# Delta rule of block 2: four inverse chains in other places, the second pair on other banks, more products queued at the start of the mixers

## The chip, the cores and the metric

One core of one Trainium2 chip runs the whole program, two transformer blocks, in one launch. The metric is device time in microseconds, the median of the runs of one kernel. The traces name the engines PE (matmul), DVE (vector), ACT (scalar), POOL (GpSimd) and SP (which issues DMAs).

## The reference, cut to what matters

Block 1 (a token mixer and sixteen experts) and the experts of block 2 are not touched. The change lies in the mixing sublayer of block 2, on 256 rows of width 1024:

```python
u_lat = modulate(rmsnorm(h_lat, norm_mix_g), m_lat[0], m_lat[1])
a_lat, b_lat, gates_lat = jnp.split(u_lat @ w_in, split_at, axis=-1)
oa = gdn_branch(a_lat, state_a, ...)      # gated delta rule, 4 heads of 128, two directions
ob = rwkv_branch(b_lat, state_b, ...)     # 8 heads of 64, two directions
y  = sigmoid(g_a) * (oa @ w_o_a) + sigmoid(g_b) * (ob @ w_o_b)
return y @ w_out
```

The delta rule is computed in chunks of 128 rows; each head and direction has two chunks:

```python
lower = where(strict, (k_beta @ k.T) * decay, 0)
a_mat = eye(128) + lower                  # its inverse is applied to the right-hand sides
for each chunk, in the direction's order:
    v_new = u_c - w_c @ s                 # u, w come from the inverse
    o_c   = q_dec @ s + qk @ v_new
    s     = s * g_end + k_dec.T @ v_new
o = rmsnorm(o_fwd + o_bwd, onorm_g) * silu(z)
```

## The kernel before

Block 2's mixers stand in one stretch, between the context's part and the merge. Three streams of work share PE there.

**rwkv** (tiles r...) goes through four head pairs, j = 0 to 3. Each has a front (products `rmt`, then two inverses, `r0ic`/`r0ib`/`r0iy` and `r1ic`/`r1ib`/`r1iy`, one for each direction) and a back, a chain of small chunk steps (`rp`), in which each step reads the state `rSU` that DVE wrote after the last; then `rbn`, `ryt`, `rgb` close the pair. Its tiles lie in the pools R and RF, its banks of PSUM are pa, pc and pd.

**gdn**, the delta rule (tiles g...), has two pairs of heads. For a pair it makes transposes and products (`gtr`, `gkk`, `gqp`, `grb`), then for each direction an inverse of seven levels: four with 32x32 blocks (`gic`, two groups of products a level: PE, then a copy or subtraction on ACT or DVE, then PE again) and two with whole tiles (`gib`, `giy`, a copy on ACT and a subtraction on DVE between), and then two state steps (`gp`), each with five groups of products that go from PE to DVE and back (`gr`, `gvn`) before the state `SA` is written. Before, pair 0 runs its two directions one after the other, both with the tiles of the pool G, and pair 1 runs them in turn, direction 0 in G and direction 1 in the pool X. X is opened when RF is closed, so it lies in RF's memory, which is free once the last rwkv pair has had its last use of it. All of gdn takes its banks from pb (two of them).

**products** are input projections that depend on nothing of the two: `gz` (the gate z of the delta rule) and sixteen columns of `pc` with the sigmoids `early` (the gates g_a and g_b). They wait in the list `waiting[1]`; `waiting[0]` holds rwkv's next pair. `advance` takes steps from a list, and `fill` does so behind a given matmul; how many steps is in the table `HOPS`. `HOPS[6]` and `HOPS[7]` are the fillers of the delta rule's inverse and state steps; before, they act on direction 0 of pair 1 only (`both and d == 0`).

The program order is rwkv whole, then gdn whole, with the fillers where the hooks put them; a scheduler then merges this into one order for each engine, which is fixed at build time. Each engine keeps its order and waits at the head of its queue. This is why gdn's pair 0, written behind all of rwkv, stands among rwkv's products in the kernel before: its places (G, pb) are free early.

**merge** follows: SP loads `w_o_b`, `w_o_a` and `w_out` (L1891), ACT and DVE or POOL split each into two parts `wp` (L290, L291), and PE makes `mo` (w_o_b half by half, L300), `gr`, `mo` again (w_o_a) and `mw` (w_out). The experts follow with 366 GB/s of weights. The normed output of the delta rule reaches the merge through `gdn_out`: ACT squares (`gjk`, `goss`), DVE scales, PE transposes (`got`). 

Of the kernel before, what the change touches and what calls it, by code (L numbers as in the profile page):

```python
# [16 lines left out]
P = 128  # L17
# [41 lines left out]
HOPS = 4, 1, (3, 1), (2, 1), (2, 1), (2, 1), (0, 4), (0, 4)  # L59
# [95 lines left out]
class Ring(list):  # L155
# [3 lines left out]
    def tile(self, *args, **kw):  # L159
        self.turn += 1  # L160
        return self[self.turn % len(self)].tile(*args, **kw)


class Net:
# [796 lines left out]
    def ctx_pre(self):  # L961
# [6 lines left out]
        with tc.tile_pool(name="CW", bufs=2, reuse_waits="tile") as CW, tc.tile_pool(name="C", bufs=1, reuse_waits="tile") as C:  # L968
# [22 lines left out]
            with tc.tile_pool(name="CG", bufs=1, reuse_waits="tile") as G:  # L991
                gates = yield from self.gdn_gates(G, uT)
                for hp in range(2):
                    qkv = []
                    yield from self.gdn_in(G, uT, False, hp, load, qkv)
                    x = yield from self.gdn_products(G, qkv, False)
                    for d in range(2):
                        yield from self.gdn_dir(G, d, False, 2 * hp, gates, x, self.SA, False, None)
# [261 lines left out]
    def gdn(self, W, gates, ins, S, o, X):  # L1260
# [80 lines left out]
    def gdn_dir(self, W, d, both, h0, gates, x, S, lat, o):  # L1341
# [8 lines left out]
        hop = (lambda *steps: (lambda ins: self.fill(ins, *steps))) if both and d == 0 else lambda *steps: (lambda ins: None)  # L1350
# [32 lines left out]
        yield from self.mixed_inverse(W, u4(N), 4, d, u4(Y), 7, "gi", hop(*HOPS[6]))  # L1383
        sl = S[d][:, h0:h0 + 2, :]
        for step in range(2):
# [5 lines left out]
            hop(*HOPS[7])(ins)  # L1391
# [7 lines left out]
            hop(*HOPS[7])(ins)  # L1399
# [4 lines left out]
            if lat:  # L1404
                p3 = half("gp3")
                for h in range(2):
                    nc.tensor.matmul(p3[:, h, :], qd[:, t, h, :], sl[:, h, :], start=True, stop=False)
                    nc.tensor.matmul(p3[:, h, :], qk[:, t, h, :], vn[:, h, :], start=False, stop=True)
                ov = o[:, t, h0 * P:(h0 + 2) * P].rearrange("p (h c) -> p h c", h=2)
                if (step if both else d) == 0:  # L1410
                    nc.scalar.copy(ov, p3)
                else:
                    nc.vector.tensor_add(ov, ov, p3)
# [9 lines left out]
    def rwkv(self, W, F, uT, S, lat, load, tags, start=None):  # L1423
# [91 lines left out]
        start()  # L1515
        for j in range(4):
# [244 lines left out]
    def lat(self):  # L1761
        tc, nc, I = self.tc, self.nc, self.I
        h = self.acc
        with ExitStack() as outer:
            L = outer.enter_context(tc.tile_pool(name="L", bufs=1, reuse_waits="tile"))
            early = [L.tile([P, KD, 256], F32, name=f"early{i}", tag=f"exp{i}") for i in range(2)]
            with self.phase(**LBANKS):
# [31 lines left out]
                with tc.tile_pool(name="R", bufs=1, reuse_waits="tile") as R, tc.tile_pool(name="G", bufs=1, reuse_waits="tile") as G, ExitStack() as mix:  # L1799
# [62 lines left out]
    def gdn_out(self, W, sz, go, oa):  # L1862
        nc = self.nc
        ss = W.tile([P, 2, 4, 2], F32, name="goss")
        for t in range(2):
            jk = W.tile([P, P], F32, name="gjk", tag="gr", padded_shape=[P, 256])
            for hh in range(4):
                nc.scalar.activation(jk, go[:, t, hh * P:(hh + 1) * P], AF.Square, accum_out=ss[:, t, hh, 0:1])
            self.rsqrt_cols(ss[:, t, :, 1], ss[:, t, :, 0], 1.0 / P, self.eps)
            for hh in range(4):  # L1870
                c = slice(hh * P, (hh + 1) * P)
                nc.vector.scalar_tensor_tensor(go[:, t, c], go[:, t, c], ss[:, t, hh, 1:2],
                                               sz[:, t, c], op0=ALU.mult, op1=ALU.mult)
        for hh in range(4):
            b = self.bank("got")
            for t in range(2):
                nc.tensor.transpose(b[:, t * P:(t + 1) * P], go[:, t, hh * P:(hh + 1) * P], self.ident)
            self.evac(oa[:, hh, :], b[:, :256], self.pc("gdn_onorm_g_2"))
# [424 lines left out]
```

## Time and profile before

| | us |
|---|---|
| median of 3 runs (lowest, highest) | 2464.67 (2458.88, 2468.92) |
| the profiled execution, whole | 2459.26 |
| its span on the core | 2457.4 |
| mixers, rwkv pairs 0 to 2 with most of gdn pair 0 (A, 1764.67 to 1969.84) | 205.17 |
| mixers, rwkv pair 3 with gdn pair 1's start (B, to 2054.90) | 85.06 |
| mixers, end of gdn pair 1, last products (C, to 2112.49) | 57.59 |
| merge up to the experts (to 2177.00) | 64.51 |

Outside the span lie 1.86 us of the profiled execution. A, B and C are cut at events of the trace: A begins where the mixers' orders begin to differ, B with the front of rwkv's pair 3, C behind its last state step, and 2112.49 is the first `mo`.

The profile is read from the whole to the part: busy shares and the granted TensorE clock by slice first, then the windows of the four stages, then in each stage what PE waited for and what its groups cost, and last the single rows in order of time. A matmul in 32-bit floats shows as two records, so that counts of the trace are twice those of the order. Matmuls overlap in the pipeline: the price of a group in a row is taken from start to start.

### The profile page before, as it was taken

Reading aid. Unit: us, or ns where it says so; the run is one execution under the profiler, and the core shown is the slowest. Engines: PE = TensorE matmul, PEld = TensorE weight load, DVE = VectorE, ACT = ScalarE, POOL = GpSimd, SP = SyncE. Lnnn points to the kernel's source line nnn. Section 1 sums busy time; section 2 is a strip of 40 time slices with the busy share of each in tenths; the row PEclk is TensorE's granted clock in tenths of the full one; section 3 lists DMA queues with packets and bytes.
Section 4 is the critical chain, followed back from the end, with each engine's and each line's share of the span. In section 5 each row is a group of like instructions: output and inputs, shape, how many; then the busy total and the mean of one; then the engine's idle time right before and its main releaser. Section 6 shows DMA issues by size and latency. Waiting matters only on the chain. (4 is left out here: it accounts for less than half of the span.)

```text
span 2457.4 us, 45180 instructions
## 1 busy us (share of the span) xinstructions
PE 2280.8 (93%) x18736; PEld 1238.1 (50%) x18736; DVE 979.8 (40%) x2419; ACT 652.7 (27%) x1652; POOL 353.7 (14%) x627
## 2 busy tenths in 40 slices
PE   7989799999999999899999999987989989989997
PEld 6756433444444443333343333325867868865554
DVE  7735311223233133232222232215576663545545
ACT  5414111211211222111122121104444433422222
POOL 3101000000000111011011011003253431300000
PEclk9989899999999999999999999998979989999999
DMA  7637999999999999999999999994211104689995
GB/s 257 213 115 262 356 395 402 402 407 406 398 400 395 366 391 405 406 408 405 406 406 404 406 407 408 406 398 115 79 39 47 52 22 145 202 278 366 366 368 181
DMA packets 318816, 755.06 MB, mean 307 GB/s; under 512 B 12944, under 2 KB 158016, under 8 KB 315536
## 3 DMA queue, kind: packets, MB, share of 16 engines
q1 hardware_dynamic: 317104, 747.67, 81.2%
q0 software_dynamic: 1504, 4.46, 0.5%
q8 instruction: 150, 2.46, 0.4%
q14 instruction: 58, 0.48, 0.1%
HBM read 751.03 MB, written 1.05 MB: 306 GB/s over the span
## 5 line engine op out<-in xcount | busy, mean ns | idle before, releaser
L909 PE MATMUL gu<-w,xs 128*64 128x512 f32 (+1 forms) x3072 | 677.7, 569 | 22.8 <-DMA w<-in_w_up 18.6
L909 PEld LDWEIGHTS gu<-w,xs 128*64 128x64 f32 x3072 | 197.1, 137 | 326.5 <-issue 257.4
L941 PE MATMUL dn<-w,hT 128*64 128x512 f32 x1408 | 336.3, 602 | 21.4 <-DMA w<-in_w_down 20.7
L1110 PE MATMUL pc<-luT,w 128*128 128x256 f32 x688 | 177.2, 399 | 2.2 <-DMA w<-in_w_in 1.5
L941 PEld LDWEIGHTS dn<-w,hT 128*64 128x64 f32 x1408 | 88.4, 136 | 176.6 <-issue 118.2
L1110 PEld LDWEIGHTS pc<-luT,w 128*128 128x128 f32 x688 | 127.3, 195 | 19.5 <-issue 1.5
L2159 PE MATMUL egu<-w,exs 128*64 128x256 f32 x1024 | 123.2, 383 | 0.0
L2159 PEld LDWEIGHTS egu<-w,exs 128*64 128x64 f32 x1024 | 74.6, 136 | 39.4 <-issue 6.9
L1692 POOL TENSOR_SCALAR rsw<-rSU,rwc 64x64 f32<-64x64 f32 x112 | 39.6, 354 | 379.1 <-DVE rSU L1708 368.9
L919 DVE TENSOR_TENSOR hid<-hid,gu 128x512 f32<-128x512 f32 (+1 forms) x48 | 30.9, 643 | 123.4 <-ACT hid L307 123.2
L920 DVE TENSOR_TENSOR hid<-hid,gu 128x512 f32<-128x512 f32 (+1 forms) x48 | 30.8, 642 | 120.4 <-PE gu L909 120.3
L1110 PE MATMUL pc<-cuT,w 128*128 128x256 f32 x288 | 71.1, 391 | 0.0
L305 ACT ACTIVATE hid<-gu 128x512 f32<-128x512 f32 (+1 forms) x48 | 26.9, 560 | 163.6 <-PE gu L909 163.4
L2186 PE MATMUL edn<-w,ehT 128*64 128x512 f32 x256 | 67.7, 597 | 0.7 <-ACT ehT L322 0.5
L1110 PEld LDWEIGHTS pc<-cuT,w 128*128 128x128 f32 x288 | 52.1, 190 | 30.8 <-issue 20.4
L291 DVE TENSOR_TENSOR wp<-w,wp 128x1024 fp32r<-128x1024 f32 (+1 forms) x44 | 57.8, 1332 | 24.2 <-ACT wp L290 24.2
L1700 DVE COPY rSU<-rp 64x64 f32<-64x64 f32 x64 | 13.5, 214 | 134.5 <-PE rp L1696 134.2
L300 PE MATMUL pj<-uTh,wp 128*128 128x272 f32 x320 | 66.0, 299 | 0.0
L1648 PE MATMUL rmt<-rT,rBK 128*128 128x128 f32 (+1 forms) x256 | 50.9, 340 | 15.3 <-DVE rT L1635 7.3
L290 ACT CAST wp<-w 128x1024 fp32r<-128x1024 f32 (+1 forms) x48 | 55.0, 1187 | 29.8 <-DMA w<-in_w_in 17.8
L1193 DVE TENSOR_TENSOR r0iB<-r0iB,r0ic 128x128 f32<-128x128 f32 x48 | 13.6, 284 | 118.5 <-PE r0ic L1172 107.2
L958 DVE SCALAR_TENSOR_TENSOR acc<-sc,aff,acc 128x512 f32<-128x512 f32 x64 | 43.7, 744 | 37.9 <-PE sc L956 37.7
(675 smaller groups left out, 3514.5 us busy)
## 6 DMA issues: line engine op xcount, KB each, us to landing
w<-in_w_down SPq DMA_DIRECT2D x176, 1024.0 KB, 16.5
w<-in_w_gate SPq DMA_DIRECT2D x128, 1024.0 KB, 17.6
w<-in_w_up SPq DMA_DIRECT2D x128, 1024.0 KB, 18.1
w<-in_w_gate SPq DMA_DIRECT2D x64, 768.0 KB, 15.8
w<-in_w_up SPq DMA_DIRECT2D x64, 768.0 KB, 14.9
w<-in_moe_w_gate SPq DMA_DIRECT2D x32, 1024.0 KB, 13.3
w<-in_moe_w_up SPq DMA_DIRECT2D x32, 1024.0 KB, 12.3
w<-in_moe_w_down SPq DMA_DIRECT2D x32, 1024.0 KB, 11.3
```

The lines of the kernel that those rows point to most:

```text
L290: self.nc.scalar.copy(hi, src)
L291: (eng or self.nc.vector).tensor_sub(lo, src, hi)
L300: self.nc.tensor.matmul(out, a[x], b[y], start=(i == 0 and x + y == 0), stop=(i == n - 1 and x == 1))
L909: ins = nc.tensor.matmul(b[h * 64:(h + 1) * 64, :w], xs[:, k, :], ws(k, slice(h * w, (h + 1) * w)), start=(k == 0), stop=(k == KD - 1))
L919: nc.vector.tensor_mul(hid, hid, gu[0][:, :w])
L941: ins = nc.tensor.matmul(dn[0][dc * 64:(dc + 1) * 64], hT[:, j, h * 64:(h + 1) * 64], wd(h * nf + j, slice(dc * 512, (dc + 1) * 512)), sta ...
L958: nc.vector.scalar_tensor_tensor(dst, b, self.aff[:, t + 1, e:e + 1], dst, op0=ALU.mult, op1=ALU.add)
L1110: self.nc.tensor.matmul(b, w(k), uT[:, k, :], start=(k == 0), stop=(k == KD - 1))
L1648: ins = nc.tensor.matmul(b[:, i], BK[:, c0 + i, h:h + 2, :], T[:, h, c0 + i, :, :], start=True, stop=True)
L1692: nc.gpsimd.tensor_scalar(sw[r], SU[r, h, c, :], wc[r, c:c + 1], 0.0, op0=ALU.mult, op1=ALU.add)
L2159: nc.tensor.matmul(b[64 * i:64 * i + 64, x * 256:x * 256 + 256], xs[:, k, i, :], w[i](k), start=(k == 0), stop=(k == KD - 1))
L2186: nc.tensor.matmul(b[64 * i:64 * i + 64, :], hT[:, j, 64 * i:64 * i + 64], wd[i](j, cs), start=(j == 0), stop=(j == 1))
```

## The change

`HOPS[0]` goes from 4 to 12 and is now used: right after the mixers' beginning twelve steps of the products' list are queued. Both pairs of gdn run their two directions in turn. Pair 0 has direction 0 in G and direction 1 in X, on the banks pb, with (0, 2) fillers in direction 0; pair 1 puts its tiles by the class `Places` into places of rwkv's pool R (and five tiles into X), on the banks pa and pc, with (0, 4) fillers as before. `gdn_out` is done pair by pair, and the transposes `got` come behind both.

```diff
-HOPS = 4, 1, (3, 1), (2, 1), (2, 1), (2, 1), (0, 4), (0, 4)
+HOPS = 12, 1, (3, 1), (2, 1), (2, 1), (2, 1), (0, 2), (0, 4)
...
+class Places:
+    COMMON = dict(gkq=("R", "rT1", [P, 3, 2, 2, P]), gkN=("X", "xkN", None), gvN=("X", "xvN", None))
+    TWO = dict(gdec="rMR", ger="rSU", gN="rN", gk2="rKt", gkd="rY", gY="r{}iB", giZ="r{}iZ", giN="r{}iN")
+
+    def __init__(self, R, X, which):
+        self.pools, self.of = dict(R=R, X=X), {}
+        if which == "products":
+            self.of = self.COMMON
+            return
+        for name, tag in self.TWO.items():
+            self.of[name] = "R", tag.format(which) if "{" in tag else tag + which, None
+        self.of["giB"] = ("R", "rT0", [P, 12, P]) if which == "0" else ("X", "xiB", None)
+        self.of["gr"] = "R", "rys" + which, None
+        self.of["gvn"] = "R", ("rbo", "rlora")[int(which)], None
...
         for hp in range(2):
-            x = run(self.gdn_products(W, ins[hp], True))
-            args = 2 * hp, gates, x, S, True, o
-            if hp == 0:
-                for d in range(2):
-                    drain(self.gdn_dir(W, d, False, *args))
-            else:
-                for _ in zip(self.gdn_dir(W, 0, True, *args), self.gdn_dir(X, 1, True, *args)):
-                    pass
+            self.ptag = cycle(("pa", "pc")) if hp else "pb"
+            x = run(self.gdn_products(W if hp == 0 else Places(R, X, "products"), ins[hp], True))
+            two = (W, X) if hp == 0 else [Places(R, X, str(d)) for d in range(2)]
+            gens = [self.gdn_dir(two[d], d, hp, 2 * hp, gates, x, S, True, o) for d in range(2)]
+            self.in_turn(("pb", "pb") if hp == 0 else ("pa", "pc"), gens)
+        for hp in range(2):
+            self.gdn_out(W, hp, sz, o)
...
-        hop = (lambda *steps: (lambda ins: self.fill(ins, *steps))) if both and d == 0 else lambda *steps: (lambda ins: None)
+        hop = (lambda *steps: (lambda ins: self.fill(ins, *steps))) if lat and d == 0 else lambda *steps: (lambda ins: None)
...
-        yield from self.mixed_inverse(W, u4(N), 4, d, u4(Y), 7, "gi", hop(*HOPS[6]))
+        yield from self.mixed_inverse(W, u4(N), 4, d, u4(Y), 7, "gi", hop(*HOPS[6 + hp]))
...
-            hop(*HOPS[7])(ins)
+            hop(*HOPS[6 + hp])(ins)
...
         start()
+
+        self.advance(self.waiting[1], HOPS[0])
         for j in range(4):
...
-                    self.ptag = "pb"
-                    self.gdn(G, self.gates, qkv, self.SA, go, X)
-                    self.gdn_out(G, sz, go, oa)
+                    self.gdn(G, self.gates, qkv, self.SA, go, X, R, sz, oa)
```

The orders of the two kernels are the same up to 1764.67 us. Where they differ is shown at three places; code lines behind the new class stand 23 to 30 higher after the change, and an x count is one of matmuls, half the records of the trace.

PE, in the front of rwkv's pair 1, where its two inverses (`r0i`, `r1i`) run. Before:

```order
L1172 MATMUL r0ic<-r0iZ,r0iB 32x32 x10
L1172 MATMUL r1ic<-r1iB 32x32 x16
L1172 MATMUL r0ic<-r0iZ,r0iB 32x32 x6
L1110 MATMUL pc<-luT,w 128x256 x2
L1200 MATMUL giy<-gY,giB 128x128 x4
L1172 MATMUL r1ic<-r1iZ,r1iB 32x32 x9
L1110 MATMUL pc<-luT,w 128x256 x2
L1172 MATMUL r1ic<-r1iZ,r1iB 32x32 x7
L1172 MATMUL r0ic<-r0iB 32x32 x16
L1110 MATMUL pc<-luT,w 128x256 x4
L1200 MATMUL gib<-giZ,giN 128x128 x4
L1172 MATMUL r1ic<-r1iB 32x32 x16
```

After, at the same place of the inverses:

```order
L1195 MATMUL r1ic<-r1iB 32x32 x16
L1195 MATMUL r0ic<-r0iZ,r0iB 32x32 x16
L1133 MATMUL pc<-luT,w 128x256 x3
L1884 MATMUL gz<-w,luT 128x128 x2
L1195 MATMUL r1ic<-r1iZ,r1iB 32x32 x16
L1223 MATMUL r0ib<-r0iZ,r0iN 128x128 x4
L1593 MATMUL rn<-rsq,stab 128x256
L1884 MATMUL gz<-w,luT 128x128 x2
L1223 MATMUL r0iy<-rY_13161,r0iB 128x128 x4
L1884 MATMUL gz<-w,luT 128x128 x2
```

Before, the last levels of gdn's pair 0 stand here (`gib`, `giy`); after, none of pair 0 does, and products `gz`, which stood later, do. Of pair 0's direction 0, after, only the two groups of the first level stand early, in the back of rwkv's pair 0; the row broadcast `grb` of direction 1 stands between them and holds a bank of pb until `gdec` of direction 1 can be written, which lies in X, and the next group of pair 0 stands behind the front of rwkv's pair 3.

PE, behind the last of rwkv's chunk steps. Before, the last pair's first state steps:

```order
L1200 MATMUL giy<-gY,giB 128x128 x4
L1390 MATMUL gp_16503<-SA_3013,gkd 128x128 x2
L1110 MATMUL pc<-luT,w 128x256 x4
L1398 MATMUL gp_16512<-gr,gY 128x128 x2
L1407 MATMUL gp_16526<-SA_3013,ger 128x128
L1110 MATMUL pc<-luT,w 128x256 x4
L1408 MATMUL gp_16526<-gvn,gdec 128x128
L1407 MATMUL gp_16526<-SA_3013,ger 128x128
L1408 MATMUL gp_16526<-gvn,gdec 128x128
L1417 MATMUL gp_16532<-gvn,gk_15999 128x128 x2
L1390 MATMUL gp_16537<-SA_3014,gkd 128x128 x2
L1398 MATMUL gp_16542<-gr,gY 128x128 x2
```

After, at the first state step of gdn's pair 0:

```order
L1418 MATMUL gp_15940<-SA_3013,gkd 128x128 x2
L1133 MATMUL pc<-luT,w 128x256 x2
L1195 MATMUL gic<-giB 32x32 x16
L1426 MATMUL gp_15952<-gr,gY 128x128 x2
L1133 MATMUL pc<-luT,w 128x256 x2
L1435 MATMUL gp_15959<-SA_3013,ger 128x128
L1195 MATMUL gic<-giZ,giB 32x32 x13
L1436 MATMUL gp_15959<-gvn,gdec 128x128
L1435 MATMUL gp_15959<-SA_3013,ger 128x128
L1436 MATMUL gp_15959<-gvn,gdec 128x128
L1445 MATMUL gp_15965<-gvn,gk_15475 128x128 x2
L1195 MATMUL gic<-giZ,giB 32x32 x3
```

Pair 0's four state steps, which before stood among rwkv's pairs 1 and 2, now stand here, between the levels of pair 1's inverses; pair 1's own state steps come behind these.

ACT, at the splits of the merge's weights (`wp`). Before, the first two casts of `w_o_b`:

```order
L1209 COPY giB<-gib 128x512
L307 ACTIVATE early_11600<-early_11600 128x256
L290 CAST wp<-w 128x2048 x2
L305 ACTIVATE early_11601<-pc 128x256
L306 ACTIVATE early_11601<-early_11601,prow 128x256
L307 ACTIVATE early_11601<-early_11601 128x256
L1411 COPY tail<-gp_16526 128x256
```

After, the first of them:

```order
L1898 ACTIVATE gjk,goss<-tail 128x128
L336 ACTIVATE goss<-goss 128x2
L1898 ACTIVATE gjk,goss<-tail 128x128
L335 ACTIVATE goss<-goss,prow 128x2
L336 ACTIVATE goss<-goss 128x2
L313 CAST moa<-tail 128x256
L313 CAST wp<-w 128x2048
L345 ACTIVATE tail<-got,pcol 128x256
L313 CAST moa<-tail 128x256 x2
```

Before, two casts stand within pair 1's inverse; after, the first stands behind the last squares of the delta rule's norm. SP's order changes with it: the second load of `w_o_b` now waits for the last `gp` that reads `gr` of pair 1, the loads of `w_o_a` for the splits of `w_o_b`, and those of `w_out` for the first products `mo` and a split of `w_o_a`.

## Rows read from the trace of the kernel before

**Rows 1.** Windows of A, B, C, merge: us, busy (records) by engine, PEclk, DMA share, GB/s

```profile
1764.67:1969.84 205.17, 189.36 (x2872) 153.20 (x2866) 135.07 (x397) 92.98 (x294) 82.53 (x152) 0.89 0.18 49
1969.84:2054.90 85.06, 74.59 (x1403) 57.90 (x1401) 45.98 (x143) 30.63 (x104) 27.20 (x49) 0.92 0.15 39
2054.90:2112.49 57.59, 55.28 (x373) 48.08 (x371) 27.58 (x58) 27.89 (x68) 6.72 (x11) 1.00 0.40 123
2112.49:2177.00 64.51, 55.84 (x371) 46.68 (x369) 37.69 (x87) 22.30 (x45) 23.16 (x8) 0.98 0.89 306
```

**Rows 2.** What PE waited for in A (two rows) and B: us, times, longest

```profile
PE rp L1711 <- DVE rSU L1700: 5.9, 6, 2.3
PE rp L1681 <- DVE rSU L1708: 5.4, 4, 2.1
...
PE r1ic L1172 <- DVE r1iB L1193: 4.1, 1, 4.1
```

**Rows 3.** Windows at the low clock, same columns as rows 1

```profile
1801.00:1813.00 12.00, 9.69 (x109) 7.43 (x110) 8.34 (x22) 3.32 (x12) 5.79 (x11) 0.51 0.00 1
1829.00:1843.00 14.00, 14.00 (x263) 9.61 (x262) 10.04 (x33) 3.40 (x11) 5.01 (x8) 0.53 0.16 44
2007.00:2014.00 7.00, 4.35 (x75) 3.54 (x76) 4.12 (x14) 1.85 (x5) 1.21 (x3) 0.52 0.00 0
```

**Rows 4.** Groups of PE in A, by line and form: records | busy, mean ns | idle

```profile
L1110 PE MATMUL pc<-luT,w 128*128 128x256 f32 x204 | 57.6, 415 | 0.0
...
L1200 PE MATMUL gib<-giZ,giN 128*128 128x128 f32 x32 | 5.7, 323 | 0.0
L1172 PE MATMUL gic<-giZ,giB 32*32 32x32 f32 x256 | 5.5, 207 | 0.0
...
L1390 PE MATMUL gp<-SA,gkd 128*128 128x128 f32 x16 | 2.8, 288 | 0.0
```

**Rows 5.** Groups of PE in B, same columns

```profile
L1110 PE MATMUL pc<-luT,w 128*128 128x256 f32 x96 | 28.9, 430 | 2.2 <-DMA w<-in_w_in 1.5 <-DVE tail L1860 0.7
...
L1172 PE MATMUL gic<-giZ,giB 32*32 32x32 f32 x212 | 4.7, 196 | 0.0
...
L1856 PE MATMUL gz<-w,luT 128*128 128x128 f32 x20 | 3.4, 285 | 0.0
```

**Rows 6.** PE in order of time, in C: start, us, group, records [idle before]

```profile
2054.87 0.54 PE L1172 MATMUL gic<-giZ,giB 32*32 32x32 f32 x38
...
2057.84 1.13 PE L1200 MATMUL gib<-giZ,giN 128*128 128x128 f32 x8 [0.28 <-DVE rmv L1737]
...
2073.21 0.61 PE L1390 MATMUL gp<-SA,gkd 128*128 128x128 f32 x4
2073.66 1.89 PE L1110 MATMUL pc<-luT,w 128*128 128x256 f32 x8
...
2079.83 0.71 PE L1390 MATMUL gp<-SA,gkd 128*128 128x128 f32 x4
...
2083.68 0.71 PE L1390 MATMUL gp<-SA,gkd 128*128 128x128 f32 x4
...
2099.58 3.69 PE L1110 MATMUL pc<-luT,w 128*128 128x256 f32 x16
2103.54 0.56 PE L1877 MATMUL got<-ctab,tail 128*128 128x128 f32 x2 [0.27 <-DVE tail L1872]
...
2112.49 0.72 PE L300 MATMUL mo<-mob,wp 128*128 128x256 f32 x4
```

**Rows 7.** SP's loads of the merge and the casts on ACT, in order of time

```profile
2061.20 1.07 SPq L1891 DMA_DIRECT2D w<-in_w_o_b  x2
...
2110.79 8.43 SPq L1891 DMA_DIRECT2D w<-in_w_out  x4
...
2070.70 3.69 ACT L290 CAST wp<-w 128x2048 fp32r<-128x2048 f32 x2
```

**Rows 8.** DMA issues between 2060 and 2140 us: count, KB each, median us to landing

```profile
w<-in_w_o_b SPq DMA_DIRECT2D x2, 1024.0 KB, 7.3
```

More of the change, by code (lines that the diff above doesn't have):

```diff
@@ L161, in tile @@
         return self[self.turn % len(self)].tile(*args, **kw)
+class Places:
[11 more added lines that the diff above has]
+        self.of["gvn"] = "R", ("rbo", "rlora")[int(which)], None
+    def tile(self, shape, dt, name, **kw):
+        pool, tag, pad = self.of[name]
+        if pad:
+            kw["padded_shape"] = pad
+        return self.pools[pool].tile(shape, dt, name=name, tag=tag, **kw)
 class Net:
@@ L997, in ctx_pre @@
                     for d in range(2):
-                        yield from self.gdn_dir(G, d, False, 2 * hp, gates, x, self.SA, False, None)
+                        yield from self.gdn_dir(G, d, 0, 2 * hp, gates, x, self.SA, False, None)
             with tc.tile_pool(name="CR", bufs=1, reuse_waits="tile") as R:
@@ L1258, in gdn_gates, with gdn @@
         return g, be, gc, gend, kdf
-    def gdn(self, W, gates, ins, S, o, X):
+    def gdn(self, W, gates, ins, S, o, X, R, sz, oa):
         for hp in range(2):
-            x = run(self.gdn_products(W, ins[hp], True))
-            args = 2 * hp, gates, x, S, True, o
-            if hp == 0:
-                for d in range(2):
-                    drain(self.gdn_dir(W, d, False, *args))
-            else:
-                for _ in zip(self.gdn_dir(W, 0, True, *args), self.gdn_dir(X, 1, True, *args)):
-                    pass
+            self.ptag = cycle(("pa", "pc")) if hp else "pb"
[5 more added lines that the diff above has]
+            self.gdn_out(W, hp, sz, o)
+        self.ptag = "pb"
+        for hh in range(4):
+            b = self.bank("got")
+            for t in range(2):
+                self.nc.tensor.transpose(b[:, t * P:(t + 1) * P], o[:, t, hh * P:(hh + 1) * P], self.ident)
+            self.evac(oa[:, hh, :], b[:, :256], self.pc("gdn_onorm_g_2"))
     def gdn_in(self, W, uT, lat, hp, load, qkv):
@@ L1339, in gdn_products, with gdn_dir @@
         return kq, kN, vN, qT, kT
-    def gdn_dir(self, W, d, both, h0, gates, x, S, lat, o):
+    def gdn_dir(self, W, d, hp, h0, gates, x, S, lat, o):
         nc = self.nc
@@ L1398, in gdn_dir @@
                 ins = nc.tensor.matmul(p2[:, h, :], Y[:, t, h, :], r[:, h, :], start=True, stop=True)
-            hop(*HOPS[7])(ins)
+            hop(*HOPS[6 + hp])(ins)
             if not lat:
@@ L1409, in gdn_dir @@
                 ov = o[:, t, h0 * P:(h0 + 2) * P].rearrange("p (h c) -> p h c", h=2)
-                if (step if both else d) == 0:
+                if step == 0:
                     nc.scalar.copy(ov, p3)
```

18 lines of the change are left out of this document (7 added, 11 removed).

## The prediction

> **What bounds the kernel now.** I read the windows of the four stages first [rows 1], then what PE waited for in them [rows 2], the granted clock in single stretches [rows 3], and the prices of groups [rows 4 to 6]. The change touches the mixers alone, and the merge and the experts hang on its end: their weight loads are released step by step by the merge. So I take everything behind the first `mo` at 2112.49 [rows 6] as one block that shifts as a whole, and ask when that `mo` starts.
>
> The three mixer stages have different limits. A (205.17 us) has PE busy for 189.36 at a mean clock of 0.89; B (85.06) 74.59 at 0.92; C (57.59) 55.28 at 1.00 [rows 1]. The reader is to see that C is full: its state steps wait for DVE all the time, but product groups `pc` stand in every gap. The slack is in A and B: 26 us of idle PE, and a low clock on top. A's largest waits are those of rwkv's back for the state `rSU`, 5.9 and 5.4 us [rows 2], which no amount of places for the delta rule shortens, since each step reads what the last one wrote. B's largest is 4.1 us for `r1iB`, when DVE is busy with the start of gdn's pair 1. [...]
>
> **What moves, counted.** Prices at the full clock, from start to start [rows 6]: a group of whole-tile products (`gib`, `giy`) 0.95 us (1.13 less its overlap with the next), a group of `gic` (32 records) 0.4 (38 records show 0.54, overlap included), a group of a state step 0.45 (2073.21 to 2073.66), a step of `pc` 0.46 (16 records, eight steps, 3.69).
>
> A loses 8 whole-tile groups (`gib` has 32 records, 4 groups, and `giy` as many), 14 of its 16 groups of `gic` (two lines of 256 records) and 15 groups of state steps (16 records, 4 groups, in L1390; 11 in the other four lines) [rows 4]: 7.6 + 5.6 + 6.8 = 20.0 us. It gains 9 steps of `pc` (111 in the new order where 204 records, 102 steps, stand now) and the 20 records of `gz` from B, 4.1 + 3: net -12.9.
>
> B loses 14.6 groups of `gic` (256 and 212 records), that `gz`, 15 steps of `pc` [rows 5], 4 groups of state steps and pair 1's 20 transposes and products at some 0.22: 5.9 + 3 + 6.9 + 1.8 + 4.4 = 22.0 us. It gains pair 0's 14 groups of `gic`, 5.6: net -16.4.
>
> C gains pair 0's 8 whole-tile groups, its 19 groups of state steps, pair 1's `gic` and its transposes and products, and 8 steps of `pc`: 7.6 + 8.6 + 5.9 + 4.4 + 3.7 = 30.2. The three balance to 1 us: no work goes away. The change moves PE work from A and B into C.
>
> **What each stage then takes.** Stage A: if work bound it, 12.9 us would go. But what is taken out was the cover of rwkv's waits, which are unchanged. I take half, -6. Bounds: -13 (all of it) and +5 (what is taken out turns into gaps, one for one, and one more stretch like 1801 to 1813 at the low clock, which costs about half its busy 9.69 us).
>
> Stage B: -16.4, the 4.1 us of waiting for `r1iB` go too, since pair 1's start leaves DVE in that stretch; about 2 us of new gaps stay in the back of pair 3, which has fewer fillers: -19. Bounds -22 and -10.
>
> Stage C is a chain, so I lay it out in three pieces. First: pair 0's two whole-tile levels, which took 15.4 us for pair 1 (2057.84 to 2073.21, with fillers) [rows 6], with pair 1's products (4.4) and 8 steps of `pc` (3.7) beside them, and behind them some 4.5 until pair 1's first `gic`, an estimate from B's DVE time for the same (the 4.1 us gap is that work): 28. Second: pair 0's four state steps. A bare one took 3.85 (2079.83 to 2083.68), one with 8 steps of `pc` in it 6.6 (2073.21 to 2079.83) [rows 6]. The new order puts 2 to 8 steps of `pc` and two or three groups of `gic` into each, and the order is strict, so I take it near the filled one: 4 x 6.5 = 26. Third: the last small levels of pair 1 with 8 steps of `pc`, 8 us; its whole-tile levels, 15.4; its state steps, bare with few fillers, 4 x 4.5 = 18; the norm and `got` up to `mo`: from 2099.58 to 2112.49 they took 12.9 us with three groups of 8 steps of `pc` (11 us) beside them, so that bare they lie between 1.9 and 12.9, and I take 5.5; and the split of `w_o_b`. Its loads were issued at 2061.20, long before their use, and the casts done by 2074.4 [rows 7]; now the second load waits for pair 1's last `gr`, takes 7.3 us to land [rows 8] and has 3.69/2 us of cast and as much subtraction behind it, against some 8 us from that `gr` to `got`: 3 us late. Sum 50.
>
> C: 28 + 26 + 50 = 104 against 57.59: +46. Bounds: +30 (only the work counts) and +57 (each of the eight state steps 1.4 us longer).
>
> The merge: `w_out` was issued at 2110.79, ahead of the first `mo` [rows 7]; in the new order it waits for the first products of `mo`, 5.7 us into them. Its use is 24 us behind the start of `mo`, and four loads take over 8.43 us to issue; so 0 to 8 us, and I take +2.
>
> Sum: -6 - 19 + 46 + 2 = +23 us. The profiled execution had 2459.26 (its span 2457.4 and 1.86 outside), which gives 2482; the median of the three runs is 5.4 us above it, which gives 2488. I set **2484**.
>
> **The rivals.** *The work is what counts* (no change). All three stages keep their present sum of gaps: A -13, B -16, C +30, merge 0 to +2: 2459 on the profiled run, 2465 on the median. For it: C's gaps are where the fillers go, and 88 steps of `pc` (40 us) stand there. Against it: in the new order hardly any fillers stand behind pair 1's second state step, where the chain is bare.
>
> *The places pay* (faster). Four chains can advance side by side; the gaps of A and B shrink: A -13, B -22, C +30, and with `gz` and products in the fronts of rwkv's pairs the low stretch 1829 to 1843 is gone (14 us at 0.53, 7 back [rows 3]): -12, 2447 to 2453. It decides if A's gaps fall below the 15.8 us of now. For it: 14.0 us busy of 14.0 in that stretch, all at half speed [rows 3]. Against it: pair 0 cannot start until X is free, so there are two chains in A, not four. [...]
>
> *The clock* (slower still). C ran at 1.00 throughout [rows 1], but the new C has bare stretches, and every low stretch of rows 3 follows such. Two like 1829 to 1843 add 14 us, and a late `w_out` 6 more: 2484 + 20 = 2504. It decides if the chains' gaps in C exceed some 2 to 4 us at once, as the one for `r1iB` did ahead of 2007 to 2014 [rows 2, 3]. [...]
>
> **How the numbers follow.** Chances: the forecast 0.45, the work rival 0.25, the places 0.15, the clock 0.15. The range takes in both outer rivals' near ends, 2449 to 2506, about 0.8. What a measurement can tell from no change is 0.5%, 12 us: slower means over 2477, faster below 2452. Forecast and clock give 0.60, of which 0.04 falls short of 2477; the work rival and that give the middle; the places give 0.15: 0.15, 0.29, 0.56.
>
> **What would show it.** The first `mo` at about 2134 instead of 2112.49, with C at 100 us or more and PE idle of 10 to 20 us in it; A some 6 us shorter with its waits for `rSU` at 11 us or more; B near 66 and without the 4 us gap; `mo` within 4 us behind the last `got`, with the split of `w_o_b` named as what ended the wait. I am wrong if C's gaps are under 5 us, if A loses all of 13 us, or if the merge grows by over 8.

## The result, and the profile after

The changed kernel is slower: 2477.29 us, median of 9 runs (2474.86 to 2479.66), against 2458.98 for the kernel before in the same count of runs (2453.80 to 2468.92). The ratio is 1.0067, its 95% interval 1.0054 to 1.0080. In the profiled executions the span went from 2457.4 to 2475.2 us, 17.8 more. The sum of the prediction (+23 on the profiled run) came near, and its direction was right, but two of its terms were wrong and in part cancelled: the mixers lost less than forecast (5.1 us against 21), and the merge lost more (12.3 against 2).

The windows of the changed kernel, cut at the same events as [rows 1] (A to the front of rwkv's pair 3, B to its last chunk step, C to the first `mo`, merge to the first `eps` of the experts); columns are us, then busy time and records of PE, PEld, DVE, ACT and POOL, the granted clock, DMA share and GB/s:

```profile
1764.67:1954.57 189.90, 169.65 (x2333) 134.26 (x2331) 115.89 (x348) 87.00 (x276) 71.12 (x141) 0.92 0.20 55
1954.57:2019.68 65.11, 59.22 (x1247) 43.51 (x1249) 37.78 (x121) 23.77 (x85) 21.86 (x44) 0.90 0.13 35
2019.68:2117.63 97.95, 87.89 (x1066) 77.39 (x1066) 49.72 (x129) 39.97 (x112) 21.27 (x28) 0.98 0.20 57
2117.63:2194.42 76.79, 61.89 (x368) 51.22 (x368) 54.03 (x87) 26.34 (x44) 22.61 (x7) 0.86 0.83 286
```

| stage | before | after | difference | forecast |
|---|---|---|---|---|
| A | 205.17 | 189.90 | -15.3 | -6 (-13 to +5) |
| B | 85.06 | 65.11 | -20.0 | -19 (-22 to -10) |
| C | 57.59 | 97.95 | +40.4 | +46 (+30 to +57) |
| merge | 64.51 | 76.79 | +12.3 | +2 (0 to +8) |
| experts, from there to the end | 280.4 | 280.8 | +0.4 | 0 |

A, B and C together are 5.1 us longer: the first `mo` starts at 2117.63 instead of 2112.49. The merge adds 12.3. The experts shift as one block, as taken.

What PE waited for in A, B, C and the merge of the changed kernel, in this order (us in total, times, the longest):

```profile
PE rbn L1753 <- DVE rbo L1751: 5.9, 2, 5.5
PE rp L1741 <- DVE rSU L1730: 5.2, 5, 2.5
PE rp L1711 <- DVE rSU L1738: 3.1, 4, 1.5
...
PE r1ic L1195 <- DVE r1iB L1211: 2.4, 1, 2.4
...
PE gp L1418 <- DVE gY L1234: 3.3, 1, 3.3
PE got L1299 <- DVE tail L1902: 2.5, 1, 2.5
...
PE mw L323 <- DVE wp L314: 4.0, 2, 3.7
PE mw L323 <- ACT wp L313: 3.7, 2, 3.4
PE mo L323 <- ACT wp L313: 1.2, 1, 1.2
```

The waits for `rSU` that DVE ended are 8.3 us where [rows 2] had 11.3; with 2.6 us more that ACT ended they are 10.9, so they are still there in full. A's largest wait, 5.5 us for `rbo`, is new. C has 10.1 us of idle PE against 2.3, and its two largest waits are the ones where a chain stands bare, that is, without filler products in its gaps: the first state step of pair 0 and the norm before `got`. The waits of the merge are new; before, `mw` waited five times for some 0.26 us.

Three stretches of the changed kernel at the low clock, and one of C at the full clock (2036 to 2044), as windows:

```profile
1812.00:1822.00 10.00, 7.61 (x53) 5.63 (x51) 6.71 (x21) 5.50 (x18) 5.47 (x13) 0.50 0.01 2
...
2036.00:2044.00 8.00, 4.65 (x38) 4.36 (x37) 7.48 (x16) 3.83 (x9) 5.09 (x4) 1.00 0.24 66
...
2116.00:2124.00 8.00, 6.51 (x29) 5.92 (x29) 6.22 (x7) 4.36 (x5) 0.58 (x1) 0.50 0.58 189
2152.00:2160.00 8.00, 3.99 (x9) 2.65 (x9) 7.79 (x11) 1.93 (x6) 4.51 (x1) 0.50 1.07 362
```

The first stands about where the kernel before had 1801 to 1813 [rows 3]. Two are new and lie in the merge: one behind the gap around `got`, one behind the gaps in `mw`, both at a granted clock of 0.50. C's largest gap, 3.35 us ahead of 2043.40, left the clock at 1.00, from 2044 to 2056 too.

PE in order of time at the places that matter, with idle time before in brackets:

```profile
2043.40 0.71 PE L1418 MATMUL gp<-SA,gkd 128*128 128x128 f32 x4 [3.35 <-DVE gY L1234]
...
2094.47 0.61 PE L1418 MATMUL gp<-SA,gkd 128*128 128x128 f32 x4
...
2117.63 2.08 PE L323 MATMUL mo<-mob,wp 128*128 128x256 f32 x8 [1.24 <-ACT wp L313]
2119.96 12.33 PE L323 MATMUL mo<-mob,wp 128*128 128x256 f32 x88 [0.25 <-DVE wp L314]
...
2145.35 0.86 PE L323 MATMUL mw<-wp 128*128 128x512 f32 x3
2149.56 0.73 PE L323 MATMUL mw<-wp 128*128 128x512 f32 x2 [3.35 <-ACT wp L313]
...
2157.36 8.14 PE L323 MATMUL mw<-wp 128*128 128x512 f32 x26 [3.68 <-DVE wp L314]
```

The first `mo` product came 2.2 us behind the start of the last `got` (2115.40) and waited for the split of `w_o_b`, as forecast. The products of w_o_b took 14.5 us (2117.63 to 2132.13) at a mean clock of 0.78, with 0.50 up to 2124, against 11.3 at 1.00. From the first `mw` to `eps` it took 49.1 us (2145.35 to 2194.42) against 40.0 (2137.00 to 2177.00). These two make the 12.3.

**Why `mw` waits.** SP issued the merge's loads late, as the order had shown:

```profile
2093.05 18.06 SPq L1916 DMA_DIRECT2D w<-in_w_o_b  x2
2119.93 3.24 SPq L1916 DMA_DIRECT2D w<-in_w_o_a  x2
2126.61 5.97 SPq L1916 DMA_DIRECT2D w<-in_w_out  x4
```

So the four splits of `w_out` on POOL ran late too, 17.1 us behind the first `mo` instead of 5.4, and now lie across the gate products' additions on DVE. First DVE, then POOL, then ACT, in the changed kernel:

```profile
2135.93 3.68 DVE L1950 TENSOR_TENSOR early<-early,early 128x256 f32<-128x256 f32 x1
...
2140.14 4.25 DVE L314 TENSOR_TENSOR wp<-early,wp 128x256 fp32r<-128x256 f32 x1 [0.20 <-ACT wp L313]
2144.31 4.76 DVE L1950 TENSOR_TENSOR early<-early,early 128x256 f32<-128x256 f32 x1
...
2149.43 0.42 DVE L1950 TENSOR_TENSOR early<-early,early 128x256 f32<-128x256 f32 x1
...
2152.35 4.62 DVE L1950 TENSOR_TENSOR early<-early,early 128x256 f32<-128x256 f32 x1
...
2134.69 14.09 POOL L314 TENSOR_TENSOR wp<-w,wp 128x2048 fp32r<-128x2048 f32 x3 [17.42 <-ACT wp L313]
2152.18 4.51 POOL L314 TENSOR_TENSOR wp<-w,wp 128x2048 fp32r<-128x2048 f32 x1 [3.39 <-ACT wp L313]
...
2149.11 0.40 ACT L313 CAST wp<-early 128x256 fp32r<-128x256 f32 x1 [7.19 <-DVE early L1950]
...
2157.00 0.40 ACT L313 CAST wp<-early 128x256 fp32r<-128x256 f32 x1 [4.29 <-DVE early L1950]
```

The same addition of 128x256 takes 0.42 us at 2149.43, when POOL is idle, and 3.7 to 4.8 while POOL splits: each long one ends about where a POOL instruction ends (three in 14.09 us, so near 2139.4, 2144.1 and 2148.8, and the last at 2156.7). Four such operations (the one at 2140.14 is the subtraction of a split, its operands in SBUF too) cost DVE 15.6 us beyond the 0.42 of each, and `mw`, which waits for their results, stands. The chain can be followed: the addition at 2144.31 ends at 2149.07, ACT's cast of its result starts at 2149.11, and the `mw` that stood for 3.35 us starts at 2149.56. The one at 2152.35 ends at 2156.97, and the split queued behind it on DVE releases the `mw` at 2157.36. POOL's splits themselves were not what `mw` waited for: by the program, the products before and behind these waits read the first two, which had ended by 2144.1; the third and fourth are for other columns. In the kernel before the same happened for 6.0 us:

```profile
2118.38 0.42 DVE L1904 TENSOR_TENSOR early<-early,mo 128x256 f32<-128x256 f32 x1 [0.98 <-PE mo L300]
...
2130.80 1.98 DVE L291 TENSOR_TENSOR wp<-early,wp 128x256 fp32r<-128x256 f32 x1 [1.81 <-ACT wp L290]
2132.70 4.83 DVE L1925 TENSOR_TENSOR early<-early,early 128x256 f32<-128x256 f32 x1
...
2117.85 9.16 POOL L291 TENSOR_TENSOR wp<-w,wp 128x2048 fp32r<-128x2048 f32 x2 [4.24 <-ACT wp L290]
2127.84 9.41 POOL L291 TENSOR_TENSOR wp<-w,wp 128x2048 fp32r<-128x2048 f32 x2 [0.83 <-ACT wp L290]
```

The reader is to see that the operation at 2118.38, whose one operand `mo` lies in PSUM, kept its 0.42 us with POOL's split running, while the one at 2132.70 with both operands in SBUF took 4.83. Before, POOL's first two splits fell into the stretch where DVE works from PSUM. That was luck of timing, and the late loads ended it. In the merges of these two traces no DVE operation that began beside a POOL split with both its operands in SBUF kept its 0.42 us: all six took 1.98 to 4.83 us, up to about the end of a split. By what means a split holds DVE back is not shown.

### The profile page after: what moved, and what is told of

Its sections match the earlier page's. It is cut to its first block, busy times and chain, and to the rows that moved or that the text cites. A ratio compares the mean times of both kernels' runs of the same rounds, so it can differ in the third digit from the quotient of the medians.

```text
span 2475.2 us, 45196 instructions
## 1 busy us (share of the span) xinstructions
PE 2283.3 (92%) x18736; PEld 1238.3 (50%) x18736; DVE 990.2 (40%) x2419; ACT 656.1 (27%) x1656; POOL 350.9 (14%) x627
## 5 line engine op out<-in xcount | busy, mean ns | idle before, releaser
L1216 DVE TENSOR_TENSOR r0iB<-r0iB,r0ic 128x128 f32<-128x128 f32 x48 | 13.6, 284 | 117.5 <-PE r0ic L1195 107.9
## 6 DMA issues: line engine op xcount, KB each, us to landing
w<-in_moe_w_down SPq DMA_DIRECT2D x32, 1024.0 KB, 11.3
w<-in_moe_w_up SPq DMA_DIRECT2D x32, 1024.0 KB, 12.3
```

## The experiments

Times of a stage are from one profiled execution of each kernel, ratios from timed runs beside the kernel before, with their 95% interval. How far one profile can be trusted is seen where several kernels have the same mixers: their first `mo` came at 2110.0 to 2112.8 in four kernels with the mixers of before, at 2114.3 and 2116.4 in two with the places alone, and at 2117.4 to 2117.9 in four with the changed mixers. So a difference of less than some 3 us at the first `mo` is not told apart by one profile each; the 5.1 us of the change are 4.6 to 7.9 by these. The first `mo`, the start of POOL's first split of `w_out` behind it, and the length of the merge by kernel:

| pair 0 | pair 1 | 12 steps queued | first `mo` | POOL's first split, behind it | merge | ratio |
|---|---|---|---|---|---|---|
| among rwkv's pairs, G | G and X (before) | no | 2112.5 | 5.4 | 64.5 | 1 |
| among rwkv's pairs, G | G and X | yes | 2126.1 | 11.3 | 69.9 | 1.0068 |
| among rwkv's pairs, G | rwkv's places | no | 2114.3 | 13.0 | 71.8 | 1.0038 |
| among rwkv's pairs, G | rwkv's places | yes | 2130.0 | 17.1 | 77.8 | 1.0098 |
| behind rwkv, G and X | rwkv's places | no | 2121.8 | 16.4 | 75.7 | 1.0104 |
| behind rwkv, G and X | rwkv's places (changed) | yes | 2117.6 | 17.1 | 76.8 | 1.0067 |
| behind rwkv, G and X | G and X | yes | 2141.2 | 11.2 | 70.3 | 1.0132 |

The merge follows the start of POOL's splits nearly in step: the later they start behind the first `mo`, the longer it is. This alone does not tell the collision from late weights; the runs on the splits below do so in part.

**Without the queue.** The changed kernel, less the line that takes twelve steps at the start:

```diff
-        self.advance(self.waiting[1], HOPS[0])
```

> The changed kernel without the twelve steps queued at the mixers' start (everything else as changed). Theory: the queued products fill the fronts of rwkv's first pairs, where low-clock stretches stood before, so part of the 15 us that stage A lost comes from them; without them A is 3 to 8 us longer and the last stage takes the products as fillers, some 2 to 5 us longer, ratio to the kernel before 1.009 to 1.011. Rival: the gain of A is only the removal of pair 0's work, and the queue is neutral: ratio 1.006 to 1.008.

Ratio 1.0104 (1.0064 to 1.0144). Its windows of A and B:

```profile
1764.67:1945.43 180.76, 161.16 (x2252) 126.51 (x2250) 114.59 (x340) 83.15 (x266) 72.77 (x141) 0.92 0.19 51
1945.43:2020.70 75.27, 64.14 (x1299) 48.80 (x1297) 40.17 (x126) 23.58 (x86) 22.22 (x44) 0.89 0.11 30
```

The ratio came where the theory put it, but for another reason: A was 9 us shorter without the queued products, not longer; B was 10 us longer and C 3. With pair 0 out of A, the queued products cost A what they weigh (PE's busy time there is 169.65 us with them and 161.16 without) and save more behind it. The first `mo` came 4.2 us later.

**Pair 0 as before, queue kept.**

```diff
-            two = (W, X) if hp == 0 else [Places(R, X, str(d)) for d in range(2)]
-            gens = [self.gdn_dir(two[d], d, hp, 2 * hp, gates, x, S, True, o) for d in range(2)]
-            self.in_turn(("pb", "pb") if hp == 0 else ("pa", "pc"), gens)
+            two = (W, W) if hp == 0 else [Places(R, X, str(d)) for d in range(2)]
+            if hp == 0:
+                for d in range(2):
+                    drain(self.gdn_dir(W, d, hp, 2 * hp, gates, x, S, True, o))
+            else:
+                gens = [self.gdn_dir(two[d], d, hp, 2 * hp, gates, x, S, True, o) for d in range(2)]
+                self.in_turn(("pa", "pc"), gens)
...
-        hop = (lambda *steps: (lambda ins: self.fill(ins, *steps))) if lat and d == 0 else lambda *steps: (lambda ins: None)
+        hop = (lambda *steps: (lambda ins: self.fill(ins, *steps))) if lat and hp and d == 0 else lambda *steps: (lambda ins: None)
...
-                if step == 0:
+                if (step if hp else d) == 0:
```

> The changed kernel with gdn's pair 0 as before: its two directions one after the other in the pool G, without fillers, so that it can run among rwkv's pairs 1 and 2; pair 1 stays in rwkv's places and on the banks pa and pc. Theory (pair 0 waiting for X is what moved 30 us of work behind rwkv): A returns to about 200 us, the last stage falls from 98 to about 70, first mo at 2112 to 2116 instead of 2117.6, and the merge stays some 10 us longer than before, since w_o_b still waits for pair 1's last tiles: ratio 1.003 to 1.006. Rival (pair 0's place does not matter, since what the last stage lost A and B gave back): the first mo stays at 2117 to 2119, ratio 1.006 to 1.008.

Theory and rival both fell. The ratio was 1.0098 (1.0063 to 1.0132), the first `mo` came at 2129.95, 12 us later than in the changed kernel:

```profile
1764.67:1986.69 222.02, 199.47 (x2909) 161.77 (x2907) 140.09 (x399) 94.69 (x299) 81.80 (x155) 0.88 0.18 48
...
2049.51:2129.95 80.44, 72.09 (x886) 61.67 (x884) 34.33 (x92) 29.27 (x81) 16.17 (x24) 0.97 0.25 69
```

C did fall, from 98 to 80, but A took 222, 17 us more than before. So holding pair 0 back was not what made the changed kernel slow; with the queue in place it was a gain of 12 us at the first `mo`. Without the queue it was a loss of 7.5 (2114.3 against 2121.8 in the table).

**The queue alone**, in the kernel before, to see whether the queue is what lengthened A:

```diff
         start()
+        self.advance(self.waiting[1], 12)
```

> The kernel before with twelve steps of the products queued at the mixers' start, and nothing else. Without them the changed kernel's first mo came 4.2 us later; with pair 0 back in G and the queue kept, A took 222 us instead of 205. Theory (the queue helps only where pair 0 is out of the way; where pair 0 runs among rwkv's pairs, 7 us of products more stand in A, and the later stages lose fillers): A 212 to 220, first mo 2114 to 2120, ratio 1.001 to 1.004. Rival (the queue is a gain by itself): first mo 2107 to 2111, ratio 0.997 to 0.999.

```profile
1764.67:1986.86 222.19, 199.50 (x2938) 161.76 (x2938) 141.41 (x403) 95.60 (x300) 82.38 (x156) 0.89 0.18 49
1986.86:2076.85 89.99, 80.45 (x1449) 61.46 (x1447) 50.05 (x146) 32.34 (x108) 27.69 (x49) 0.87 0.16 43
2076.85:2126.14 49.29, 46.73 (x287) 41.16 (x287) 22.17 (x53) 24.11 (x61) 6.53 (x11) 1.00 0.38 120
```

Ratio 1.0068 (1.0051 to 1.0084), beyond the theory's range, as are A and the first `mo`. A is 17 us longer, the same 222 as in the last kernel, B is 5 longer, and only C gets 8 back. Of A's 17 us, 10.1 are busy time of PE and 6.9 idle time. By tiles, the queued products are 6.6 us of the busy time (20 records more of `pc` and 20 of `gz`), and the same 440 records of rwkv's `rp` take 4.1 us more (48.3 against 44.2). B lost its 20 records of `gz` but took 44 of `gic` from C and 18 more of `pc`, at a mean clock of 0.87 against 0.92; its idle time did not grow (9.5 against 10.5 us). So the queue costs 13.6 us at the first `mo` where pair 0 runs among rwkv's pairs, and saves 4.2 where it does not. Why rwkv's steps in A then take longer and wait more was not taken further apart.

**Places alone**: pair 0 as before, no queue, only pair 1 in rwkv's places and on pa and pc. These are the lines shown for pair 0 as before, and one more:

```diff
-        self.advance(self.waiting[1], HOPS[0])
```

> The kernel with pair 0 as before (in G, one direction after the other), no queued products, and only pair 1 moved to rwkv's places and to the banks pa and pc. Theory (the queue lengthened A in the kernel with pair 0 in G): A 205 to 212, first mo 2114 to 2122 since pair 1 still starts behind rwkv, merge 75 to 78 by the late weights: ratio 1.006 to 1.009. Rival (moving pair 1 alone costs the 17 us): first mo at 2126 or later, ratio 1.009 to 1.012.

```profile
1764.67:1968.71 204.04, 188.25 (x2849) 152.28 (x2849) 133.91 (x394) 92.44 (x294) 82.53 (x152) 0.89 0.17 47
1968.71:2029.82 61.11, 52.41 (x864) 39.85 (x862) 33.24 (x110) 24.27 (x90) 17.14 (x37) 0.94 0.10 28
2029.82:2114.31 84.49, 79.63 (x906) 68.63 (x907) 38.81 (x91) 32.34 (x84) 17.38 (x25) 0.92 0.30 84
2114.31:2186.11 71.80, 58.41 (x370) 48.72 (x369) 49.01 (x87) 25.82 (x47) 22.62 (x7) 0.93 0.85 298
```

Ratio 1.0038 (1.0024 to 1.0051), under both ranges, and the merge is shorter than the theory's 75 to 78. A is as before; B gives 24 us, C takes 27: moving pair 1 behind rwkv costs the mixers 1.8 us, which one profile does not tell from nothing, and the rest, 7.3, is the merge.

**The changed kernel without the places**: both pairs in G and X, on pb:

```diff
-            self.ptag = cycle(("pa", "pc")) if hp else "pb"
-            x = run(self.gdn_products(W if hp == 0 else Places(R, X, "products"), ins[hp], True))
-            two = (W, X) if hp == 0 else [Places(R, X, str(d)) for d in range(2)]
+            self.ptag = "pb"
+            x = run(self.gdn_products(W, ins[hp], True))
+            two = W, X
...
-            self.in_turn(("pb", "pb") if hp == 0 else ("pa", "pc"), gens)
+            self.in_turn(("pb", "pb"), gens)
```

> The changed kernel without the class Places: both pairs run their directions in turn in G and X, on the banks pb, so pair 1 waits for pair 0's tiles; queue and fillers as changed. w_o_b is then free of pair 1's tiles. Theory (the places let pair 1's small levels run beside pair 0's state steps, and they are also what makes the merge late): last stage 110 to 122 us instead of 98, first mo at 2130 to 2142, merge 64 to 68 us instead of 77: ratio 1.004 to 1.008. Rival (the last stage is bound by its work, 88 of 98 us, places or not): first mo at 2116 to 2122, merge 64 to 68: ratio 1.001 to 1.003.

Ratio 1.0132 (1.0117 to 1.0147), over the theory's range; the first `mo` at 2141.19 and C, 120 us, are as the theory had them, C 22 more than with the places. The largest wait of PE in it:

```profile
PE gic L1195 <- POOL giB L1210: 15.5, 2, 8.9
```

That is the start of pair 1's inverse, bare. The merge did not return to 64 to 68 although `w_o_b` came early (issued at 2025.5); it took 70.3, with three DVE operations of 4.2 to 4.8 us in it. `w_out` was still late, issued 3.9 us behind the first `mo` where the kernel before has 1.7 us ahead of it. That spoke for the collision, and against a late `w_o_b` as the only cause.

**The splits of w_out on DVE**, in the changed kernel:

```diff
-        wo = [parts(w, nc.gpsimd) for w in ws[:2]]
+        wo = [parts(w, nc.vector) for w in ws[:2]]
...
-                wo += [parts(w, nc.gpsimd) for w in ws[2:]]
+                wo += [parts(w, nc.vector) for w in ws[2:]]
```

> The changed kernel with the four splits of w_out subtracted on DVE (2.3 us each) instead of POOL (4.6 us each). In the changed kernel's trace four DVE operations of 0.42 us on SBUF operands took 3.7 to 4.8 us, each ending with the end of a POOL split. Theory: DVE is held by POOL's splits, and mw waits for DVE; without POOL the long operations vanish, the two waits of 3.4 and 3.7 us ahead of mw go and with them the low-clock stretch behind: merge 6 to 10 us shorter, ratio 1.003 to 1.004. Rival: mw waits for the late loads themselves, the splits only follow: merge within 2 us, ratio 1.006 to 1.008.

Ratio 1.0026 (1.0010 to 1.0043). The merge, one of the additions that had been long, and the one wait of `mw` that is left:

```profile
2117.41:2187.66 70.25, 59.35 (x368) 50.77 (x369) 46.56 (x91) 26.32 (x44) 4.01 (x3) 0.91 0.90 311
...
2144.48 0.42 DVE L1950 TENSOR_TENSOR early<-early,early 128x256 f32<-128x256 f32 x1
...
2149.16 8.91 PE L323 MATMUL mw<-wp 128*128 128x512 f32 x38 [1.65 <-DVE wp L314]
```

All of these additions take 0.42 us again, the merge is 6.5 us shorter, and DVE is busy for 7.5 us less though it has 9 us of splits more. The mixers are unchanged (first `mo` at 2117.41). The collision is shown: without it three fifths of the change's cost go by the ratios, and 7.3 of 17.8 us by the spans (2475.2 and 2467.9). It is not the whole of the merge's loss. The merge is still 5.7 us longer than before: its first products take 14.4 us against 11.3, at a mean clock of 0.79, and `mw` now waits for DVE, whose own late splits stand between the additions. And the kernel before gains by the same two lines, as is shown below.

**Other buffers for w_out's loads**, so that they don't wait for `mo`, in the changed kernel:

```diff
-            self.raws = Ring([rr])
-            self.rings = Ring([rr] * 4 + [re] * 3 + [rd] * 5 + [rr] * 2 + [ring] * 3 + [re])
+            self.raws, self.raws2 = Ring([rr]), Ring([rd])
+            self.rings = Ring([rr] * 4 + [re] * 3 + [rd] + [rr] * 2 + [ring] * 3 + [rd] * 4 + [re])
...
-        def raw(name, k0, cs):
-            t = kv(self.raws.tile([P, SLOTW], F32, name="w", tag="w"), 4, 512)
+        def raw(name, k0, cs, raws=self.raws):
+            t = kv(raws.tile([P, SLOTW], F32, name="w", tag="w"), 4, 512)
...
-        ws = [raw("w_out_2", k0, cs) for cs in halves for k0 in (0, 4)]
+        ws = [raw("w_out_2", k0, cs, self.raws2) for cs in halves for k0 in (0, 4)]
```

> The changed kernel with the four raw loads of w_out in other buffers (those free early), so that they no longer wait for the first products mo; splits stay on POOL. Theory A (the loads' time sets the merge): loads issued before 2118 instead of 2126 to 2132, mw without its 3.4 and 3.7 us waits, ratio 1.002 to 1.004. Theory B (the collision of DVE with POOL sets it, whenever the splits run): the long DVE operations move to the splits of w_o_a or the gate products but remain three or four, merge 0 to 5 us shorter, ratio 1.005 to 1.007.

Ratio 1.0063 (1.0046 to 1.0079), the number of theory B, though not by its mechanism. The loads were issued at 2111.5, one long DVE operation was left (4.65 us), and `mw`'s waits were down to 0.3 each, as A had it. But `w_o_a` now stood behind `w_out` on the queue and landed later (its first cast began at 2134.05, in the changed kernel at 2124.92), and `mo` waited instead:

```profile
PE mo L323 <- ACT wp L313: 4.1, 2, 2.9
```

The merge was 3.7 us shorter in the profile, and hardly anything in the timed runs.

**Both repairs together**, in the changed kernel, by the last two diffs:

> The changed kernel with both repairs of the merge: w_out's loads in buffers that are free early, and its splits subtracted on DVE. If the merge's 12 us are the collision and the late loads together, and the mixers' 5 us stay, the first mo comes at 2117 to 2118, the merge takes 64 to 68 us and the ratio is 1.001 to 1.003. Rival (the merge is slow by the late w_o_b and the low clock behind the last got, which neither repair touches): merge 69 us or more, ratio as with the splits on DVE alone, 1.0025 to 1.004.

Ratio 1.0052 (1.0032 to 1.0072), beyond both ranges, merge 73.7: longer than with the DVE splits alone (70.25), though the intervals of the two ratios overlap. From the first `mo` to `mw` it took 32.6 us, where with the DVE splits alone it took 27.6: `w_o_a` landed late again (first cast at 2134.03). The rival's number for the merge was nearer, its cause was not what the trace shows.

**The DVE splits in the kernel before**, twice, by the same two lines changed from `nc.gpsimd` to `nc.vector`:

> The kernel before with the splits of w_out subtracted on DVE instead of POOL. Before, two DVE operations were held by POOL (1.98 and 4.83 us for 0.42), and mw waited five times for some 0.26 us. Theory of the collision: merge 1 to 3 us shorter, ratio 0.9985 to 0.9995. Rival (DVE's own 9 us of splits delay the gate products more than POOL did): merge equal or longer, ratio 1.000 to 1.002.

> The kernel before with w_out's splits on DVE once more, since the first interval, 0.9974 to 1.0001, just took in no change. Theory of the collision: ratio 0.998 to 0.9995, upper end of the interval below 1. Rival (no gain): interval around 1.

Ratios 0.9988 (0.9974 to 1.0001) and 0.9983 (0.9969 to 0.9997). The merge of the second:

```profile
2112.78:2174.69 61.91, 54.41 (x371) 47.15 (x369) 39.09 (x91) 22.17 (x45) 4.59 (x4) 0.96 0.92 318
```

It took 61.9 us in both, 2.6 us less than in [rows 1]. This version beats both kernels, by a little: the second interval lies below 1, the first just takes it in.

So the collision cost 6.5 us of the merge in the changed kernel and 2.6 in the kernel before; what the change added to it is nearer 4 us, a difference of differences of single profiles. With DVE's splits in both kernels the change's merge is still 8.3 us longer (70.25 against 61.91): 3.1 in the first products (14.4 against 11.3) and 5.2 from `mw` on (42.6 against 37.4). By the ratios some 0.004 of the 0.0067 is left. So the merge loses in other ways too: by the low clock behind the bare end of C (0.79 in the first products), and by splits that come late whichever engine makes them (`mw` waited 1.65 us for one of DVE's). How the 5.2 us divide is not shown.

**Both repairs in the kernel before**, by the same lines as in the changed kernel:

> The kernel before with the same two repairs. Splits on DVE alone gave 0.9988. If earlier loads of w_out help where w_o_b is early too, merge 58 to 61 us and ratio 0.996 to 0.998; rival (w_out's loads now pass ahead of w_o_a's on the queue and mo waits instead): 0.9985 to 1.001.

Ratio 0.9992 (0.9978 to 1.0006), merge 65.7: in the profile the other buffers for w_out cost again what the DVE splits gave. The ratio lies in the rival's range, but `mo` did not wait here; what was lost lies behind the first 48 products of `mw`: PE waited 1.8 us there for DVE's `acc`, and the next 18 products took 5.99 us at a mean clock of 0.71, where with the DVE splits alone they took 4.37. Why DVE was later is not shown.

**Places alone, with the DVE splits**, which is the kernel of places alone with the two lines `nc.gpsimd` changed to `nc.vector`:

> Pair 0 as before, no queued products, pair 1 in rwkv's places, and w_out's splits on DVE. The first mo of this kernel without the DVE splits came at 2114.3 and its merge took 71.8. If that merge is the collision again: merge 64 to 67, ratio 1.000 to 1.002. Rival (late loads, low clock): merge 69 to 72, ratio 1.003 to 1.004.

```profile
2116.40:2181.18 64.78, 55.06 (x370) 47.06 (x368) 42.43 (x91) 25.75 (x47) 4.01 (x3) 0.98 0.95 332
```

Ratio 0.9994 (0.9979 to 1.0009). Here `w_out` comes late too (issued 5.9 us behind the first `mo`), and the merge is 64.8, 7.0 less than with POOL's splits, with `mw` waiting for 0.5 us in all. Beside the kernel before with the same splits (61.9) 2.9 us of loss are left. So for pair 1's places the collision was the larger part of the merge's loss of 7.3, and not all of it.

## Why the prediction was right, and where its steps failed

The direction and the size held: +18.3 us on the medians, where +23 was summed, inside the range. That it came so near is luck: the mixers were forecast 15.9 us too long and the merge 10.3 too short. The time it set, 2484, also rests on the median of three runs, 2464.67, which nine runs put at 2458.98. By the prediction's own signs, two of the three that would show it wrong came true (A lost more than 13 us, the merge grew by over 8), and the first `mo`, forecast at about 2134, came at 2117.63. What it had right are the direction, the work that moves, B, and that C pays.

**What moves** held. The three counts (A -12.9, B -16.4, C +30.2) are seen in PE's busy time, -19.7, -15.4 and +32.6, where A's surplus goes with its higher clock (0.92 against 0.89).

**Stage A** was mis-sized: -15.3, past the bound of -13. The step that failed was taking half of the moved work for lost in gaps. Idle time grew by 4.4 us only (15.8 to 20.3), and the time at the low clock fell, which the sum had as a cost and not as a gain. An estimate from the windows, with the slow time taken at half speed as in [rows 3] (0.51 to 0.53): a mean of 0.89 over 205 us is some 45 us at half speed, 0.92 over 190 some 30, which is 7 us back. -12.9 + 4.4 - 7 is -15.5. The 14 us at the low clock from 1829 on [rows 3] are down to some 7 (1837 to 1844, at 0.51), half of what the rival of the places had said of them, and these stand behind the new wait for `rbo`. The rest of the gain lies in other stretches.

**Stage B** held at -20.0 against -19. The wait for `r1iB` shrank from 4.1 to 2.4 us instead of going.

**Stage C** was 98 instead of 104. Its pieces: 23.7 us to the first state step of pair 0 (28 forecast, to a point 3 us later), 28.7 for pair 0's four state steps with pair 1's small levels in between (26), and 45.6 from there (50). Pair 1's first state step stood at 2094.47, ahead of the last whole-tile level of its other direction, so that some 6 us were counted twice. The filled price of a state step, 6.5, was near (28.7 / 4 = 7.2).

**The merge** was mis-sized, +12.3 past a bound of 8. The prediction had the late loads and the 3 us of the split ahead of `mo`. It had not asked what runs beside the splits when they move: DVE's additions from SBUF, which took 3.7 to 4.8 us instead of 0.42 beside POOL's splits. The row for it was in the trace of before (4.83 us for an addition that takes 0.42) and was not read. Without POOL's splits the changed kernel's merge is 6.5 us shorter. The sum had also put no price on the low clock behind the bare norm, which made the first products 3.2 us longer (14.5 us at a mean clock of 0.78, 11.3 at 1.00).

**The rivals.** That only the work counts is refuted: mixers with the same work took from 348 to 377 us in the kernels above. The places alone brought no gain to the mixers (+1.8). The clock rival had new low stretches behind bare ones, which came (0.50 from 2116 to 2124 and from 2152 to 2160), but the wrong stage: C ran at 0.98, they are in the merge. Its measure, a gap of 2 to 4 us at once, was the author's estimate and did not decide either: 3.35 us ahead of 2043.40 left the clock at 1.00, and 2.5 us ahead of `got` were followed by the stretch at 0.50. Nor were all the low stretches of [rows 3] thin: from 1829 to 1843 PE was busy for 14.0 of 14.0 us.

What stays open is why twelve queued steps stretch A by 17 us where pair 0 runs there, and what makes up the merge's loss from `mw` on that is left without the collision.

## What to carry to other kernels

When a change delays a load, follow what the load's consumers will then run beside, not only whether it is in time: here the splits on POOL began 17 us behind the first product instead of 5, and slid into DVE's additions; taking them off POOL gave 6.5 us back (2.6 in the kernel before), while the move of the mixers cost 5.1. Three edits of one change can have opposite signs by pairs, so they are worth trying singly and in twos: the queue cost 13.6 us in one setting and saved 4.2 in the other. An operation whose longest instance is ten times its median (4.83 us against 0.42 in the trace of before) is a question to ask of the trace before anything is moved.

## What the hardware showed that was not expected

In these traces a DVE operation with both operands in SBUF was held until the end of the POOL split that ran, and was let in between two of them, so that beside a row of POOL splits of 4.5 to 4.7 us DVE did about one such operation for each: 4.25 and 4.76 us in a row for 0.42. The same operation with one operand in PSUM was not touched (0.42 us at 2118.38). On DVE the split itself took 2.29 us, half of POOL's 4.5 to 4.7, so that here POOL gave no relief: moving four splits onto DVE made DVE's busy time in the changed kernel's merge shorter, 46.6 against 54.0 us, since the profile counted the time in which DVE was held as busy (4.76 us for the addition at 2144.31).
